# S5 products out of the state: four bands of 32 columns in two places of 96 records, read back on SyncE's queue

## The chip, the cores and the metric

The kernel runs on one core of a Trainium2 chip. The metric is the device time of one execution in microseconds, the median of several executions. The engines are named as in the profile: PE is TensorE (matmuls), DVE VectorE, ACT ScalarE, POOL GpSimd, SP SyncE (which here only issues DMAs).

## The reference

The network has two layers. A layer is a gated feed-forward part, a mixer, and a second gated feed-forward part, each on a normalised and modulated input, for 128 context tokens and 256 latent tokens (384 in all) of 1024 features. The change is in the mixer, whose input projection feeds three branches:

```
z = h @ w_in                                  # 512 + 512 + 512 columns
y_a = s5(z_a);  y_b = conv(z_b);  y_c = chunk_mlp(z_c)
gates = sigmoid(h @ w_gate + b_gate)          # 3 x 1024 columns
merged = g_a * (y_a @ w_br_a) + g_b * (y_b @ w_br_b) + g_c * (y_c @ w_br_c)
return merged @ w_out

def s5(z):                                    # 32 groups g of 16 channels, state of 64, both directions
    h[t] = abar_g * h[t-1] + bbar_g @ u[t]    # complex, forward; and the same backward
    y = sum over directions of Re(c_g @ h) + d * z
    y = gelu(y)
    return y * sigmoid(y @ w_glu)
```

All is float32. The three outputs are those of the context tokens, of the latent tokens, and the last S5 states of the context.

## The kernel before, in words

**Products.** Features lie on the partitions and the 384 tokens in the free dimension. A weight matrix is read in *units* of four k-tiles by 256 columns (128 x 1024 elements; those of w_br_c and w_br_b have two k-tiles, 128 x 512). A unit passes through four engines: SyncE loads it (`wr`, line 149), ScalarE rounds it to a short form (`wh`, L126), VectorE takes the rest (`wl` = `wr` - `wh`, L105), and TensorE makes three products for each k-tile and half of the columns (`mm3`, L198 to L200): `wh` by the high part of the input, `wh` by the low part, `wl` by the high part. There are three buffers each of `wr`, `wh` and `wl`, so the load of a unit may start when the `wl` three units earlier is made, and a `wh` when TensorE is done with the unit three before.

**Order in the mixer.** After w_in come the gate's third quarter and w_br_c by turns (two gate units, one of w_br_c, four times), then eight units of gate and so on. Beside this stream runs the rest of the mixer, written in `side()` as a plan with one step for each unit; its TensorE work goes into a queue `small` of *places*. After each `mm3` one place is taken from that queue and its matmuls stand there, between the large ones. TensorE's order is that in which the code is written. On the other engines, and in SyncE's queue of DMA issues, a scheduler at build time fixes the order. Each engine, and each queue, is then worked off strictly in that order.

**S5.** The 32 groups go in four quarters q of eight groups (GB = 8, GS = 4), and the 384 tokens as NCH = 48 chunks of TC = 8 tokens, so that a group's 16 channels times 8 tokens fill 128 partitions. For a quarter:

- `load_to(q)`: SyncE loads the rotation `m_rot`, the factors `m_rho` and two matrices `m_ms` (L1171).
- `to_state(q)`: the chunk's contribution to the state, `m_ms` by `U`, in two places (real and imaginary part), in four bands of 32 columns; ScalarE copies the result to `m_xs`.
- `rotate`, `scan`: VectorE turns the sequences (`m_t`), runs the recurrence as two scans over 400 elements, and turns back to `m_hh`.
- `load_from(q)`: SyncE loads `m_my` (two) and `m_mi` (L1254).
- `from_state(q)`: the output, `m_mi` by `U` and `m_my` by `m_hh`, summed in PSUM. ScalarE copies it out and writes it to `y_d` in DRAM; GpSimd reads it back as `m_yt`.
- `activate(t)`: adds d * z, applies gelu, and splits the result in `ah` and `al`, the input of the glu product.

The convolution's 31 taps for two halves (`cacc`, L123) are VectorE's filler between these.

Of the kernel before, what the change touches and what calls it, by code (L numbers as in the profile page):

```python
# [19 lines left out]
P = 128  # L20
# [36 lines left out]
def hybrid_step(ctx: ExitStack, tc: tile.TileContext, I, pos_r, pos_c, y_prompt, y_sample, new_state):  # L57
# [37 lines left out]
    def c2(shape, name):  # L95
        return sp.tile(shape, F32, tag="c2", name=name, bufs=7)
# [1021 lines left out]
    def mixer(l, ld, nxt):  # L1118
# [11 lines left out]


        zd = drm.tile([G, H, TC, NCH], F32, tag=f"z_d{l}", name="z_d")
        yd = drm.tile([NT, G * H], F32, tag=f"y_d{l}", name="y_d")
        ld.start()
        hs = ld.hs
        zp = m6([P, 4, NT], "zp")
# [43 lines left out]
        def to_state(q):  # L1180
            d = st5[q]
            gs = slice(q * GB, (q + 1) * GB)
            XS = c3([P, 2, GB, NE], "m_xs")
            d["xs"] = XS
            pool.memset(XS[:, :, :, 0:1], 0.0)
            act.activation(XS[:, :, :, EC], h0[:, :, gs], AF.Copy)

            def product(i, g, b):
                for r in range(0, P, 32):
                    pe.matmul(  # L1190
                        b[r : r + 32, g * NCH : (g + 1) * NCH],
                        d["ms"][g // GS][:, g % GS, i, r : r + 32],
                        U[:, q * GB + g, :],
                        start=True,
                        stop=True,
                        skip_group_check=True,
                    )

            def take(i, b):
                bv = b[:, : GB * NCH].rearrange("p (g c) -> p g c", c=NCH)  # L1200
                act.activation(XS[LO, i, :, 1:EC], bv[LO, :, :CC], AF.Copy)
                act.activation(XS[LO, i, :, EC + 1 :], bv[LO, :, CC:], AF.Copy)
                act.activation(XS[HI, i, :, 1:EC], bv[HI, :, CC - 1 :: -1], AF.Copy)
                act.activation(XS[HI, i, :, EC + 1 :], bv[HI, :, NCH - 1 : CC - 1 : -1], AF.Copy)

            for i in range(2):
                b = tb_bank()
                small.append([partial(product, i, g, b) for g in range(GB)] + [partial(take, i, b)])

        def rotate(q, part):  # L1210
            d = st5[q]
# [44 lines left out]
        def from_state(q):  # L1256
            d = st5[q]
            hh, mib = d["hh"], d["mi"]
            b = tb_bank()

            def product(g):
                for n in range(3):
                    for half in range(2):
                        i = 4 * half + g
                        u = U[:, q * GB + i, :] if n == 0 else hh[:, n - 1, i, :]
                        w = mib[:, i, :] if n == 0 else d["my"][i // GS][:, i % GS, n - 1, :]
                        pe.matmul(
                            b[64 * half : 64 * half + NCH, g * P : (g + 1) * P],
                            u,
                            w,  # L1270
                            start=(n == 0),
                            stop=(n == 2),
                            skip_group_check=True,
                        )

            def take():
                ysb = c2([P, TC, 4, H], "m_ysb")
                bv = b.rearrange("p (g i h) -> p i g h", g=4, h=H)
                yv = yd.rearrange("(c i) f -> c i f", i=TC)
                for half in range(2):  # L1280
                    r = slice(64 * half, 64 * half + NCH)
                    act.activation(ysb[r], bv[r], AF.Copy)
                    f0 = q * P + 64 * half
                    bq.dma_start(yv[:, :, f0 : f0 + 64], ysb[r].rearrange("c i g h -> c i (g h)"))
                d["yt"] = c2([P, 3, P], "m_yt")
                gq.dma_start(d["yt"], yd[:, q * P : (q + 1) * P].rearrange("(t p) f -> p t f", p=P))

            small.append([partial(product, g) for g in range(4)] + [take])

        def activate(t):  # L1290
            b = tb_bank()
            for n in range(3):
                transpose(b[:, n * P : (n + 1) * P], st5[t]["yt"][:, n, :], P)
            y2 = tmp("y2")
            ci = lambda v: v.rearrange("p (c i) -> p c i", i=TC)
            stt(ci(y2), zp[:, t].rearrange("p (j c) -> p c j", j=TC), pv[:, 48 + t : 49 + t], ci(b[:, :NT]))
            ga = tmp("ga")
            gelu_sig(ga, y2)
            yg = zp[:, t]
            mul(yg, y2, ga)  # L1300
            ygs[t] = yg
            hl = a_pair()
            split(yg, *hl)
            yas[t] = hl
# [183 lines left out]
        def side():  # L1488
            f = lambda fn, *a: (fn, a)
            tap = [f(conv_taps, j, min(j + 3, CONV_K)) for j in range(0, CONV_K, 3)]  # L1490
            plan = [
                [f(sg_weights)],
                [],
                [f(sg_bias)],
                [f(sg_u, 0), f(sg_u, 1)],
                [f(sg_gelu)],
                [f(to_state, 0), f(sg_norm)],
                [f(load_from, 0), f(rotate, 0, 0), f(rotate, 0, 1)],
                [f(load_to, 1), f(scan, 0, 0), f(sg_mix), f(sg_out)],
                [f(scan, 0, 1)],  # L1500
                [f(to_state, 1), tap[0]],
                [f(load_to, 2), f(rotate, 1, 0), f(rotate, 1, 1)],
                [f(from_state, 0), f(load_from, 1), f(scan, 1, 0)],
                [f(scan, 1, 1)],
                [f(to_state, 2), tap[1]],
                [f(load_to, 3), f(rotate, 2, 0), f(rotate, 2, 1)],
                [f(from_state, 1), f(load_from, 2), f(scan, 2, 0)],
                [f(scan, 2, 1)],
                [f(to_state, 3), tap[2]],
                [f(rotate, 3, 0), f(rotate, 3, 1)],  # L1510
                [f(from_state, 2), f(load_from, 3), f(scan, 3, 0)],
                [f(scan, 3, 1), f(activate, 0)],
                [tap[3]],
                [f(activate, 1)],
                [f(from_state, 3), tap[4]],
                [f(ctx_states), tap[5]],
                [f(activate, 2)],
                [tap[6]],
                [tap[7]],
                [f(activate, 3), tap[8]],  # L1520
                [tap[9]],
                [tap[10]],
                [f(conv_mean)],
                [f(conv_center)],
                [],
                [f(conv_var)],
                [],
                [f(conv_bcast)],
                [f(conv_scale)],
                [f(conv_out)],  # L1530
            ]
            for step in plan:
                for fn, a in step:
                    fn(*a)
                yield
# [312 lines left out]
```

## Time and profile before

| | |
|---|---|
| time before, median of 3 runs | 1773.07 us (1772.1 to 1774.9) |
| the profiled execution | 1772.74 us |
| its span in the trace | 1770.9 us |
| granted clock of TensorE, mean | 0.994 |
| TensorE busy | 98% |
| VectorE busy | 71% |
| ScalarE busy | 45% |
| GpSimd busy | 11% |

Busy shares are averages over the whole span; the mixer of the first layer lies around 350 to 570 us, that of the second 865 us later. In a timeline, a row is one instruction or a run of equal ones, with its start, its length, the engine, the line and what it makes from what; in brackets stands how long the engine sat idle before it and what released it. A letter q behind an engine's name (SPq) is its DMA issues. The matmuls of a place appear as two records each.

### The profile page before, as it was taken

How to read it: one execution, taken by the hardware profiler on the slowest of the kernel's cores; microseconds unless marked ns; L12 is line 12 of the kernel's file. 1: busy time of each engine (PE TensorE's matmuls, PEld its weight loads, DVE VectorE, ACT ScalarE, POOL GpSimd, SP SyncE). 2: the span in 40 equal slices, each digit the busy share in tenths (PEclk: the TensorE clock that was granted, in tenths of full speed). 3: DMA queues.
4: the chain of work that ended last, by engine and by line, in shares of the span. 5: the costliest groups of instructions: out<-in, count | busy, mean ns of one | idle time of the engine just before them, and what ended most of it. 6: DMA issues, size and time to landing. Idle time of an engine off the chain costs nothing.

```text
span 1770.9 us, 31161 instructions
## 1 busy us (share of the span) xinstructions
PE 1739.2 (98%) x12244; PEld 1660.3 (94%) x12244; DVE 1249.3 (71%) x2352; ACT 795.7 (45%) x1332; POOL 202.6 (11%) x400
## 2 busy tenths in 40 slices
PE   6999999999999999999999999999999999999997
PEld 4989989999999999999999999999999999999997
DVE  5495776888986986657787666677699688544445
ACT  3344333475355553233367333335744546323233
POOL 2012333410010000000001133222100000000000
PEclk9999999999999999999999999999999999999999
DMA  9679787676753567766745577757666443444342
GB/s 358 209 234 317 251 261 213 204 213 188 251 150 102 185 223 247 255 197 219 250 131 184 174 220 233 244 172 236 167 209 195 131 126 113 135 128 128 122 125 77
DMA packets 250298, 344.49 MB, mean 195 GB/s; under 512 B 22016, under 2 KB 216268, under 8 KB 250153
## 3 DMA queue, kind: packets, MB, share of 16 engines
q1 hardware_dynamic: 225048, 299.18, 53.1%
q0 software_dynamic: 17088, 39.51, 7.4%
q10 hardware_dynamic: 8016, 3.82, 0.8%
q8 instruction: 96, 1.57, 0.4%
q14 instruction: 50, 0.40, 0.1%
HBM read 309.75 MB, written 32.70 MB: 193 GB/s over the span
## 4 chain that ended last, share of the span: by engine, by line
PE 84%; DVE 10%; DMA 2%; ACT 2%; issue 1%; DVEq 0%; SPq 0%; ACTq 0%
PE mm L198 26%; PE mm L200 26%; PE mm L199 26%; PE ax L356 3%; DVE wl L105 2%; DVE cacc L123 2%; PE tb L138 1%; DVE m_t L105 1%; DMA wr<-in_w_in_dram 1%; DVE m_hh L105 1%; DMA wr<-in_w_gate_dram 1%; ACT wh L126 1%; PE tb L1042 0%; DMA modw<-in_w_mod_dram 0%; DVE acc L105 0%
## 5 line engine op out<-in xcount | busy, mean ns | idle before, releaser
L105 DVE TENSOR_TENSOR wl<-wr,wh 128x1024 fp32r<-128x1024 f32 (+2 forms) x389 | 457.0, 1175 | 335.7 <-ACT wh L126 333.9
L126 ACT ACTIVATE wh<-wr 128x1024 fp32r<-128x1024 f32 (+1 forms) x387 | 395.9, 1023 | 629.1 <-PE mm L199 444.6
L198 PE MATMUL mm<-hh,wh 128*128 128x384 f32 x1840 | 625.7, 340 | 5.0 <-ACT hh L639 5.0
L200 PE MATMUL mm<-hh,wl 128*128 128x384 f32 x1840 | 618.6, 336 | 5.7 <-DVE wl L105 5.5
L199 PE MATMUL mm<-hl,wh 128*128 128x384 f32 x1840 | 617.7, 336 | 0.2
L198 PEld LDWEIGHTS mm<-hh,wh 128*128 128x128 f32 x1840 | 347.2, 189 | 21.8 <-ACT wh L126 7.5
L200 PEld LDWEIGHTS mm<-hh,wl 128*128 128x128 f32 x1840 | 347.0, 189 | 8.3 <-DVE wl L105 8.2
L199 PEld LDWEIGHTS mm<-hl,wh 128*128 128x128 f32 x1840 | 347.2, 189 | 1.1 <-DVE hl L105 1.0
L198 PE MATMUL mm<-ah,wh 128*128 128x384 f32 x800 | 273.1, 341 | 0.0
L200 PE MATMUL mm<-ah,wl 128*128 128x384 f32 x800 | 270.1, 338 | 0.0
L199 PE MATMUL mm<-al,wh 128*128 128x384 f32 x800 | 269.4, 337 | 0.0
L198 PEld LDWEIGHTS mm<-ah,wh 128*128 128x128 f32 x800 | 150.3, 188 | 6.4 <-ACT wh L126 2.3
L199 PEld LDWEIGHTS mm<-al,wh 128*128 128x128 f32 x800 | 150.4, 188 | 0.6
L200 PEld LDWEIGHTS mm<-ah,wl 128*128 128x128 f32 x800 | 150.2, 188 | 0.0
L123 DVE SCALAR_TENSOR_TENSOR x<-mm,gt,x 128x128 f32<-128x128 f32 x224 | 83.3, 411 | 37.2 <-PE mm L200 37.1
L123 DVE SCALAR_TENSOR_TENSOR macc<-modw,silu_c,macc 128x1024 f32<-128x1024 f32 x56 | 70.0, 1279 | 21.4 <-DMA modw<-in_w_mod_dram 21.4
L198 PE MATMUL mm<-xh,wh 128*128 128x386 f32 x240 | 84.0, 350 | 0.0
L199 PE MATMUL mm<-xl,wh 128*128 128x386 f32 x240 | 81.4, 339 | 0.0
L200 PE MATMUL mm<-xh,wl 128*128 128x386 f32 x240 | 81.3, 339 | 0.0
L126 ACT ACTIVATE ah<-av 128x384 fp32r<-128x384 f32 x82 | 41.9, 517 | 82.3 <-DVE av L105 82.2
L123 DVE SCALAR_TENSOR_TENSOR cacc<-pad,pv,cacc 128x399 f32<-128x399 f32 x120 | 69.6, 627 | 0.0
L105 DVE TENSOR_TENSOR av<-mm,sg 128x384 f32<-128x384 f32 x76 | 42.1, 555 | 23.3 <-PE mm L200 23.0
(315 smaller groups left out, 1838.9 us busy)
## 6 DMA issues: line engine op xcount, KB each, us to landing
wr<-in_ffn_w_dram SPq DMA_DIRECT2D x256, 512.0 KB, 3.8
modw<-in_w_mod_dram SPq DMA_DIRECT2D x56, 768.0 KB, 5.7
modw<-in_w_mod_dram SPq DMA_DIRECT2D x56, 512.0 KB, 4.6
wr<-in_w_gate_dram SPq DMA_DIRECT2D x48, 512.0 KB, 3.6
wr<-in_w_in_dram SPq DMA_DIRECT2D x24, 512.0 KB, 4.6
my<-my POOLq DMA_DIRECT2D x16, 512.0 KB, 5.5
ms<-ms POOLq DMA_DIRECT2D x16, 512.0 KB, 5.5
m_ms<-ms SPq DMA_DIRECT2D x16, 512.0 KB, 7.0
```

Source lines behind the costliest of these rows:

```text
L105: (eng or dve).tensor_tensor(out, a, b, op=op)
L123: dve.scalar_tensor_tensor(out, a, s, b, op0=op0, op1=op1)
L126: act.activation(hi, full, AF.Copy)
L138: pe.transpose(out, in_, ident[:rows, :rows])
L198: pe.matmul(out, wh[:, k, cols], xh, start=first, stop=False)
L199: pe.matmul(out, wh[:, k, cols], xl, start=False, stop=False)
L200: pe.matmul(out, wl[:, k, cols], xh, start=False, stop=last)
L356: pe.matmul(b[32 * s : 32 * s + 32, :w], silu_c[:, k, :], raw[:, s * w : s * w + w], start=(k == 0), stop=(k == KD - 1), skip_group_check= ...
```

## The change

- `to_state`: both parts (real, imaginary) go into one place of the queue, 64 matmuls in a row.
- `from_state`: before, the stationary operand was `U` or `m_hh` (48 columns) and the moving one `m_mi` or `m_my` (128 columns), in one place of four steps. Now the stationary operand is a band of 32 columns of `m_mi` or `m_my` and the moving one `U` or `m_hh` (48 columns), in two places, four groups each. The result lies transposed to that of before.
- ScalarE copies one 128 x 384 block in place of two of 48 x 512, and writes `y_d` with one DMA in place of two.
- `load_y(q)`, new: `m_yt` is read with eight DMAs of 16 x 8 x 48 for each quarter, on SyncE's queue, in place of one DMA on GpSimd's. The plan has a step for it.
- `activate`: the three transposes are gone, since `m_yt` already lies with channels on the partitions; `y` is made from SBUF; the last multiply writes its result in token order.

```diff
-        yd = drm.tile([NT, G * H], F32, tag=f"y_d{l}", name="y_d")
+        yd = drm.tile([4, P, GB, NCH], F32, tag=f"y_d{l}", name="y_d")
...
+            place = []
             for i in range(2):
                 b = tb_bank()
-                small.append([partial(product, i, g, b) for g in range(GB)] + [partial(take, i, b)])
+                place += [partial(product, i, g, b) for g in range(GB)] + [partial(take, i, b)]
+            small.append(place)
...
                 for n in range(3):
-                    for half in range(2):
-                        i = 4 * half + g
-                        u = U[:, q * GB + i, :] if n == 0 else hh[:, n - 1, i, :]
-                        w = mib[:, i, :] if n == 0 else d["my"][i // GS][:, i % GS, n - 1, :]
+                    u = U[:, q * GB + g, :] if n == 0 else hh[:, n - 1, g, :]
+                    w = mib[:, g, :] if n == 0 else d["my"][g // GS][:, g % GS, n - 1, :]
+                    for r in range(0, P, 32):
                         pe.matmul(
-                            b[64 * half : 64 * half + NCH, g * P : (g + 1) * P],
+                            b[r : r + 32, g * NCH : (g + 1) * NCH],
+                            w[:, r : r + 32],
                             u,
-                            w,
...
-                ysb = c2([P, TC, 4, H], "m_ysb")
...
-                d["yt"] = c2([P, 3, P], "m_yt")
-                gq.dma_start(d["yt"], yd[:, q * P : (q + 1) * P].rearrange("(t p) f -> p t f", p=P))
-
-            small.append([partial(product, g) for g in range(4)] + [take])
+                ysb = c2([P, GB, NCH], "m_ysb")
+                act.activation(ysb, b[:, : GB * NCH].rearrange("p (g c) -> p g c", c=NCH), AF.Copy)
+                bq.dma_start(yd[q], ysb)
+
+            small.append([partial(product, g) for g in range(GS)])
+            small.append([partial(product, g) for g in range(GS, GB)] + [take])
+
+        def load_y(q):
+            d = st5[q]
+            d["yt"] = c2([P, TC, NCH], "m_yt")
+            for g in range(GB):
+                tq.dma_start(d["yt"][g * H : (g + 1) * H], yd[q, :, g, :].rearrange("(i h) c -> h i c", h=H))
...
-            for n in range(3):
-                transpose(b[:, n * P : (n + 1) * P], st5[t]["yt"][:, n, :], P)
             y2 = tmp("y2")
...
-            mul(yg, y2, ga)
+            mul(yg.rearrange("p (c i) -> p i c", i=TC), jc(y2), jc(ga))
...
-                [f(to_state, 2), tap[1]],
+                [f(to_state, 2), f(load_y, 0), tap[1]],
...
-                [f(to_state, 3), tap[2]],
+                [f(to_state, 3), f(load_y, 1), tap[2]],
...
-                [f(activate, 1)],
+                [f(load_y, 2), f(activate, 1)],
...
-                [f(activate, 2)],
+                [f(load_y, 3), f(activate, 2)],
```

SyncE's queue, before, in the first layer's mixer, from the load of c4 (the last unit of w_br_c in it) on; the two `m_ms` behind it are those of quarter 3, and the gate units that follow are g9 to g14:

```order
L149 DMA wr<-in_w_br_c_dram 128x2x256
L1171 DMA m_ms<-ms_128 128x1024 x2
L149 DMA wr<-in_w_gate_dram 128x4x256 x2
L1251 DMA m_my<-my_130 128x1024 x2
L1254 DMA m_mi<-mi_134 128x1024
L149 DMA wr<-in_w_gate_dram 128x4x256 x2
L1251 DMA m_my<-my_130 128x1024 x2
L149 DMA wr<-in_w_gate_dram 128x4x256 x2
L1254 DMA m_mi<-mi_134 128x1024
```

The same queue now, from the gate unit g9 on (g9, g10, g11 and g12 are its four loads):

```order
L149 DMA wr<-in_w_gate_dram 128x4x256
L1289 DMA m_yt<-y_d 16x8x48
L1165 DMA m_rot<-rot_136 128x800
L149 DMA wr<-in_w_gate_dram 128x4x256
L1167 DMA m_rho<-rhod_138 128x400
L1171 DMA m_ms<-ms_128 128x1024 x2
L1253 DMA m_my<-my_130 128x1024
L149 DMA wr<-in_w_gate_dram 128x4x256
L1253 DMA m_my<-my_130 128x1024
L149 DMA wr<-in_w_gate_dram 128x4x256
L1256 DMA m_mi<-mi_134 128x1024
```

The two `m_ms` of quarter 3 stood right behind c4 and now stand behind g10; the `m_mi` of quarter 2 stood behind g10 and now behind g12. Further on, from g13 to g16, the queue now reads:

```order
L149 DMA wr<-in_w_gate_dram 128x4x256
L1289 DMA m_yt<-y_d 16x8x48
L149 DMA wr<-in_w_gate_dram 128x4x256
L1289 DMA m_yt<-y_d 16x8x48 x4
L1253 DMA m_my<-my_130 128x1024
L149 DMA wr<-in_w_gate_dram 128x4x256
L1253 DMA m_my<-my_130 128x1024
L149 DMA wr<-in_w_gate_dram 128x4x256
L1256 DMA m_mi<-mi_134 128x1024
```

The `m_mi` of quarter 3, before behind g14, now stands behind g16, and reads of `m_yt` stand between the weight loads.

VectorE, before, from the `wl` of c3 (between the gate units g6 and g7) to that of g7, in the first layer; numbers in the names `m_t` tell buffers of a quarter apart:

```order
L105 TENSOR_TENSOR wl<-wr,wh 128x512
L123 SCALAR_TENSOR_TENSOR cacc<-pad,pv_311,cacc 128x399
L105 TENSOR_TENSOR m_t_5325<-m_rot,m_xs 128x400
L123 SCALAR_TENSOR_TENSOR cacc<-pad,pv_311,cacc 128x399 x2
L105 TENSOR_TENSOR m_t_5326<-m_rot,m_xs 128x400
L105 TENSOR_TENSOR m_t_5327<-m_rot,m_xs 128x400
L105 TENSOR_TENSOR m_t_5325<-m_t_5325,m_t_5326 128x400
L105 TENSOR_TENSOR m_t_5328<-m_rot,m_xs 128x400
L1233 SCALAR_TENSOR_TENSOR m_t_5326<-m_rho,m_t_5325 128x400
L105 TENSOR_TENSOR m_t_5327<-m_t_5327,m_t_5328 128x400
L105 TENSOR_TENSOR m_t_5325<-m_rot,m_t_5326 128x400
L105 TENSOR_TENSOR wl<-wr,wh 128x1024
```

The same stretch now, from the `wl` of g6 over those of c3 and g7 to that of g8 and what follows:

```order
L105 TENSOR_TENSOR wl<-wr,wh 128x1024
L105 TENSOR_TENSOR acc<-mm,gt 128x384
L105 TENSOR_TENSOR wl<-wr,wh 128x512
L105 TENSOR_TENSOR acc<-mm,gt 128x384
L123 SCALAR_TENSOR_TENSOR cacc<-pad,pv_311,cacc 128x399 x11
L105 TENSOR_TENSOR wl<-wr,wh 128x1024
L123 SCALAR_TENSOR_TENSOR cacc<-pad,pv_311,cacc 128x399 x6
L105 TENSOR_TENSOR wl<-wr,wh 128x1024
L123 SCALAR_TENSOR_TENSOR cacc<-pad,pv_311,cacc 128x399
L105 TENSOR_TENSOR acc<-mm,gt 128x384
L123 SCALAR_TENSOR_TENSOR cacc<-pad,pv_311,cacc 128x399 x2
L105 TENSOR_TENSOR m_t_5402<-m_rot,m_xs 128x400
```

The rotation and the first scan of quarter 2 (`m_t`) stood ahead of the `wl` of g7; now taps of the convolution stand there, and the rotation comes behind the `wl` of g8.

## Rows read from the trace of the kernel before

**Rows 1.** Windows: us, busy time (count) of PE, PEld, DVE, ACT, POOL, clock, DMA share, GB/s.

```profile
411.00:522.00 111.00, 108.34 (x1111) 102.87 (x1110) 110.36 (x208) 48.63 (x90) 8.86 (x16) 1.00 0.61 195
...
1276.00:1387.00 111.00, 107.98 (x1109) 102.52 (x1108) 110.34 (x208) 48.71 (x90) 3.96 (x8) 1.00 0.59 192
```

**Rows 2.** Timeline of PE: places, waits, and the first glu product.

```profile
462.44 0.89 PE L1190 MATMUL tb<-U,m_ms 128*32 128x48 f32 x64
...
470.86 0.45 PE L200 MATMUL mm<-hh,wl 128*128 128x384 f32 x1 [0.25 <-DVE wl L105]
...
488.60 0.45 PE L200 MATMUL mm<-hh,wl 128*128 128x384 f32 x1 [1.35 <-DVE wl L105]
...
493.14 0.43 PE L1267 MATMUL tb<-m_mi,U 128*48 128x128 f32 x4
...
531.27 0.65 PE L198 MATMUL mm<-ah,wh 128*128 128x384 f32 x1
```

**Rows 3.** Timeline of PE: three kinds of places and the matmuls around them.

```profile
403.53 0.34 PE L200 MATMUL mm<-hh,wl 128*128 128x384 f32 x1
...
403.79 0.89 PE L1190 MATMUL tb<-U,m_ms 128*32 128x48 f32 x64
...
404.89 0.33 PE L199 MATMUL mm<-hl,wh 128*128 128x384 f32 x1
...
432.44 0.43 PE L1267 MATMUL tb<-m_mi,U 128*48 128x128 f32 x4
...
435.47 0.33 PE L199 MATMUL mm<-hl,wh 128*128 128x384 f32 x1
...
477.76 0.49 PE L138 MATMUL tb<-ident,m_yt 128*128 128x128 f32 x3
...
478.26 0.34 PE L199 MATMUL mm<-hl,wh 128*128 128x384 f32 x1
```

**Rows 4.** Timeline of SyncE's queue.

```profile
449.72 0.88 SPq L1171 DMA_DIRECT2D m_ms<-ms  x2
...
462.34 0.38 SPq L1254 DMA_DIRECT2D m_mi<-mi  x1
...
480.40 0.45 SPq L1254 DMA_DIRECT2D m_mi<-mi  x1
```

**Rows 5.** Timeline of VectorE.

```profile
447.39 1.81 DVE L105 TENSOR_TENSOR wl<-wr,wh 128x1024 fp32r<-128x1024 f32 x2
...
453.19 0.98 DVE L1233 TENSOR_TENSOR_SCAN m_t<-m_rho,m_t 128x400 f32<-128x400 f32 x1
...
459.58 1.23 DVE L105 TENSOR_TENSOR wl<-wr,wh 128x1024 fp32r<-128x1024 f32 x1
...
463.35 1.25 DVE L105 TENSOR_TENSOR m_hh<-m_t,m_t 64x128 f32<-64x128 f32 x4
...
501.46 6.63 DVE L123 SCALAR_TENSOR_TENSOR cacc<-pad,pv,cacc 128x399 f32<-128x399 f32 x12
...
508.00 1.22 DVE L105 TENSOR_TENSOR wl<-wr,wh 128x1024 fp32r<-128x1024 f32 x1
...
511.31 0.90 DVE L123 SCALAR_TENSOR_TENSOR y<-zp,pv,tb 128x384 f32<-128x384 f32 x1
...
523.39 0.56 DVE L105 TENSOR_TENSOR al<-zp,ah 128x384 fp32r<-128x384 f32 x1 [0.59 <-ACT ah L126]
```

**Rows 6.** DMAs from issue to landing: first of the tile m_ms, then of m_mi.

```profile
DMA to landing us min/median/max: 4.7/7.0/8.6
...
DMA to landing us min/median/max: 5.6/7.0/8.3
```

**Rows 7.** Timeline of PE behind a long wait, and a window there.

```profile
43.28 0.69 PE L198 MATMUL mm<-hh,wh 128*128 128x384 f32 x1 [3.05 <-ACT hh L639]
...
49.31 0.48 PE L200 MATMUL mm<-hh,wl 128*128 128x384 f32 x1
...
43.00:46.00 3.00, 2.67 (x7) 2.27 (x8) 2.88 (x9) 1.90 (x5) 0.00 (x0) 0.50 1.02 386
```

More of the change, by code (lines that the diff above doesn't have):

```diff
@@ L1276, in take @@
             def take():
-                ysb = c2([P, TC, 4, H], "m_ysb")
[L1278 to L1284, printed above, removed]
-                d["yt"] = c2([P, 3, P], "m_yt")
-                gq.dma_start(d["yt"], yd[:, q * P : (q + 1) * P].rearrange("(t p) f -> p t f", p=P))
-            small.append([partial(product, g) for g in range(4)] + [take])
+                ysb = c2([P, GB, NCH], "m_ysb")
[8 more added lines that the diff above has]
+                tq.dma_start(d["yt"][g * H : (g + 1) * H], yd[q, :, g, :].rearrange("(i h) c -> h i c", h=H))
         def activate(t):
-            b = tb_bank()
-            for n in range(3):
-                transpose(b[:, n * P : (n + 1) * P], st5[t]["yt"][:, n, :], P)
             y2 = tmp("y2")
-            ci = lambda v: v.rearrange("p (c i) -> p c i", i=TC)
-            stt(ci(y2), zp[:, t].rearrange("p (j c) -> p c j", j=TC), pv[:, 48 + t : 49 + t], ci(b[:, :NT]))
+            stt(y2, zp[:, t], pv[:, 48 + t : 49 + t], st5[t]["yt"].rearrange("p i c -> p (i c)"))
             ga = tmp("ga")
```

## Prediction

> **What bounds the kernel now.** I read the windows first: over the middle of the mixer TensorE is busy 108.34 of 111 us in the first layer and 107.98 in the second, with VectorE busy 110.36 and 110.34 [rows 1]. The reader is to see two engines full at once: TensorE's own work is the time, and VectorE has nothing to spare in exactly the stretch that the change touches. Next the timeline of TensorE: it still stands 0.25 us ahead of the place of from_state(2) and 1.35 us later on, both times for `wl`, which VectorE makes [rows 2]. So a microsecond less on TensorE counts only where VectorE and the loads follow; and an order that makes VectorE or SyncE later can cost at once. The second layer repeats the first 864.97 us later, so I work out one mixer and double it. The profiled execution took 1772.74 us (span 1770.9 and 1.8 around it), 0.3 under the median; all sums start from 1772.7.
>
> **TensorE's own work.** A place of 64 records of to_state costs 403.79 to 404.89 less one usual spacing of 0.173: 0.93 us, and it begins 0.09 later than a matmul would [rows 3]. Two of them become one of 128: one start is saved, between 0 and 0.2 us; I take 0.2, since the start is seen in every place. from_state's 48 records cost 2.86 (432.44 to 435.47) [rows 3]. The new form, four bands of 32 columns with 48 moving ones, is to_state's form, which runs 64 records in 0.93: 96 records are 1.39, two places 2.79, plus one more start of 0.09. That is 2.88 for 2.86: nothing gained. Each activate loses three transposes, 0.33 us (477.76 to 478.26 less a spacing) [rows 3]. A quarter gives 0.53 us, a layer 2.1, both 4.2.
>
> The Trainium skill ("TensorE: Matmul & The Clock Gate", section "Wait — 56ns, not 53.3ns?") says that matmuls never start less than about 25 ns apart, however small. By that 96 records would be 2.4 us and a quarter 2.1 us dearer than now, some 17 us in all, as an estimate. The place of 64 records shows 14.5 ns a record, so here the measurement decides: the records of different bands run beside each other.
>
> **Work that is hidden.** The copy out of PSUM and the one write in place of two lie on ScalarE, which is not full (48.63 of 111 us [rows 1]). The eight reads of a quarter cost SyncE some 0.4 us each (an issue there takes 0.38 [rows 4]); they stand between weight loads that wait for VectorE anyway, until the order below. `y` reads 384 contiguous elements: I take 0.5 us in place of the 0.82 of now (0.90 at 511.31, [rows 5]), and the multiply into `zp` may pay that back; between them 0.3 gained and 0.35 lost, hidden, since the last `al` ends 8 us before the glu products (523.39 and 531.27 [rows 2, 5]). That margin is also what an 8 us delay of activate(3) alone would eat.
>
> **What is moved, and costs.** The orders shown with the change are the heart. SyncE is one queue: a load behind a weight load waits until that may start, and `wr` of a unit may start when VectorE has made `wl` three units earlier. I call the gate units g1 to g20 and the w_br_c units c1 to c4; each c stands behind every second g, so g10 waits for g8, g12 for g9 and g16 for g13. Before, both `m_ms` of quarter 3 are issued from 449.72, behind c4; now they stand behind g10 and m_rho. `m_mi` of quarter 2 goes from behind g10 (462.34) to behind g12, that of quarter 3 from behind g14 (480.40) to behind g16 [rows 4].
>
> So VectorE's new order sets them. From its rows a full `wl` costs 1.13 us (1.22 less the 0.09 by which durations overlap), a half one 0.59 (with a full one it makes the 1.81 at 447.39), a tap 0.545 (twelve from 501.46 to 508.00), a scan 0.90, a group of four m_hh 1.25, a 384-wide operation 0.47 and a 400-wide one 0.485 (an estimate by width) [rows 5]. `wl` of g6 starts near 447.0 (before 447.39: two acc go behind it, a tap goes ahead). Then 1.72 for it and c3, two acc 0.94, eleven taps 6.0: g7 at 455.7; 1.13 and six taps 3.27: g8 from 460.1 to 461.2. That is before's time (459.58 [rows 5]) almost exactly; but now the loads of `m_ms` stand behind it. Issues: g10 461.2, m_rho 461.6, m_ms 462.1 and 462.6.
>
> From 461.2 follow a tap, acc, two taps, five 400-wide operations, scan, two, scan, half `wl`, one, acc, m_hh, fin: 10.2 us, so `wl` of g9 runs 471.4 to 472.5, and g12 and m_mi(2) are issued at 472.6 and 473.0. To g13 follow twelve 400-wide operations 5.8, five taps 2.7, three m_hh 3.8, two scans 1.8, three `wl` 3.4, and acc, y, ga, zp, fin 3.2: 20.7 us. So g13 runs 493.2 to 494.4; g16 and m_mi(3) at 494.4 and 494.9.
>
> **The sum, for a layer.** (1) to_state(3): TensorE is there at 461.9 (462.44 [rows 2], less 0.4 by which `wl` of g6 comes sooner and 0.1 of places before). An m_ms lands 4.7 to 8.6 us after issue, median 7.0 [rows 6]; I take 6.5 for the second, since two loads go ahead of the pair: 469.1, with bounds 467.3 and 471.2. It is needed from the second half of the first 64 records on; 96 records remain, 1.4 us. TensorE leaves at 470.5, where before the same work was done at 464.3 (462.44 and two places): 6.2 late.
>
> (2) The clock. In the trace TensorE waited 3.05 us before 43.28, and the granted clock behind it is 0.50, which is 1.2 GHz; the 18 matmuls to 49.31 take 6.03 us where 18 spacings of 0.173 are 3.1: 2.9 lost [rows 7]. The wait of 1.35 us did no such thing: the granted clock of the whole stretch around it is 1.00 [rows 1, 2]. A wait of near 7 us is more than either, so I add 2.5 (0 to 2.9): 8.7. The wait of 0.25 goes [rows 2]: 8.45 late at from_state(2), which before starts at 471.2; so 479.7. m_mi lands 5.6 to 8.3 after issue [rows 6]; only one weight load stands just ahead of it, so I take 5.6: 478.6, in time. At the median of 7.0 it costs 0.4 more.
>
> (3) Between from_state(2) and from_state(3) two activates save 0.66 in transposes, and the 1.35 us wait goes, whose `wl` is early now: 6.4 late, from_state(3) at 499.6 (493.14 before [rows 2]). m_mi(3), again with one weight load ahead, lands at 500.5 (500.5 to 503.2): 0.9 of wait, 7.4 late. This load is a floor too: if less is lost before it, TensorE only waits longer for it.
>
> (4) Behind it two activates save 0.66: 6.7 late at the glu products. Behind them I know of no wait that could give it back. Twice 6.7 is 13.4: 1772.7 + 13.4 = **1786.1 us**.
>
> **Rivals.** *A. The loads stall TensorE (above), 1781 to 1793.* For it: the queue is in order, and VectorE has no gap in which it could reach g8 sooner. Chance 0.74.
>
> *B. The loads come in time, and VectorE's order alone paces.* If m_ms(3) landed by 462, from_state(2) would need m_hh of quarter 2, which the new order ends at 475.3 (2.8 us behind `wl` of g9): 4.1 late, less 1.35 and four times 0.33 behind it: 1.4 a layer, 1775.5; with the clock falling in that wait, 2.5 more a layer, 1780.5. Against it: issue to landing never went under 4.7 us [rows 6]. Chance 0.09.
>
> *C. Faster: the work saved on TensorE reaches the end.* One mechanism: VectorE runs the taps and `wl` ahead of g8 some 7 us faster than its rows give, and m_ms(3) is issued before 455.5, the point from which it decides. Then 2.1 a layer is gained, 1768.5, and with the two waits gone [rows 2] 1765.3. Against it: VectorE is busy 110.36 of 111 us [rows 1]. Chance 0.08.
>
> *D. The clock stays down.* If it fell at each of the three late loads (quarter 3 in, quarters 2 and 3 out), at 2.9 each, a layer costs 5 to 6 more: 1796 to 1798. The waits before the latter two are 0 and 0.9 in my sum, and 1.35 did nothing. Chance 0.06.
>
> *E. The bands don't run beside each other.* The row nearest is from_state's own: 2.86 us for 48 records with 128 moving columns, 60 ns each; 48 columns by that are 22 ns, a place 2.15, a quarter 1.4 dearer, 11 us over eight: 1797. Against it: the same form in to_state at 14.5 ns. Chance 0.03. (The skill's 25 ns above would be this case, and a little worse.)
>
> **Range and chances.** 1786.1 is A's value. About 0.2% (3.5 us) is what a measurement here can tell from no change. Downwards the floor of m_mi(3) holds it; there only VectorE's sum, which I give 2.5 us over the 47 of it, a layer, counts: 1781. Upwards m_mi(3) at 503.2 or m_ms(3) at 471.2 with the clock at 2.9 add 2.5 to 3.5 a layer: 1793. With half of B and little of D, 1777 to 1794 holds eight in ten. Faster by over 0.2%: C, 0.08. Within: part of B and the bottom of A, 0.06. Slower: 0.86.
>
> **What the profile after would show.** Right: TensorE idle 6 to 8 us ahead of to_state(3), near 462 and again 865 us later, released by the load of m_ms, with granted clock 0.50 behind it; m_ms(3) issued near 462 instead of 449.7; m_mi(2) near 473 and m_mi(3) near 495; a place of from_state of 1.4 us; the 1.35 us wait gone. Wrong if m_ms(3) is issued well before 460, if `wl` of g8 is reached at another time than 460, if a place takes 2 us, or if the stall at to_state(3) is there and is caught up before the glu products.

## The result, and the profile after

The changed kernel takes 1788.2 us (median of 4 runs, 1785.0 to 1793.7) against 1774.0 (1772.1 to 1775.1): a ratio of 1.009, 95% interval 1.0076 to 1.0104. It is slower, by 14 us; 1786.1 was forecast. The profiled execution, the fastest of the four, took 1785.0 us (span 1783.2), 12.2 more than that of before; what follows explains those 12.2.

First the waits of TensorE in the changed kernel (what it waited for: us in all, how many times, the longest). Before, it had none of these; it had 5.5 us of waits for `wl`, which are gone.

```profile
PE tb L1190 <- DMA m_ms<-ms: 11.7, 4, 7.1
PE tb L1268 <- issue: 5.3, 4, 2.0
...
PE tb L1268 <- DMA m_mi<-mi: 3.4, 3, 2.1
```

Next its timeline: to_state(3), the first product of c4, from_state(3) and the first glu product of the first layer, then to_state(3) and the first glu product of the second layer.

```profile
462.31 0.34 PE L200 MATMUL mm<-hh,wl 128*128 128x384 f32 x1
466.61 0.87 PE L1190 MATMUL tb<-U,m_ms 128*32 128x48 f32 x32 [3.96 <-DMA m_ms<-ms]
467.80 2.15 PE L1190 MATMUL tb<-U,m_ms 128*32 128x48 f32 x96 [0.33 <-DMA m_ms<-ms]
469.88 0.69 PE L198 MATMUL mm<-hh,wh 128*128 128x384 f32 x1
...
474.69 0.33 PE L198 MATMUL mm<-yc,wh 128*128 128x384 f32 x1
...
500.02 0.29 PE L1268 MATMUL tb<-U,m_mi 128*32 128x48 f32 x7 [2.14 <-DMA m_mi<-mi]
...
536.70 0.65 PE L198 MATMUL mm<-ah,wh 128*128 128x384 f32 x1
...
1340.66 0.87 PE L1190 MATMUL tb<-U,m_ms 128*32 128x48 f32 x32 [7.05 <-DMA m_ms<-ms]
...
1408.67 0.65 PE L198 MATMUL mm<-ah,wh 128*128 128x384 f32 x1
```

And before, the first product of c4 in the first layer and the first glu product of the second:

```profile
468.03 0.33 PE L198 MATMUL mm<-yc,wh 128*128 128x384 f32 x1
...
1396.24 0.65 PE L198 MATMUL mm<-ah,wh 128*128 128x384 f32 x1
```

The reader is to see: to_state(3), which ran at 462.44 without a wait before [rows 2], stands still for 3.96 and 0.33 us in the first layer and 7.05 and 0.33 in the second, each time for `m_ms`. The glu products start at 536.70 instead of 531.27 [rows 2]: 5.4 late, and 12.4 late in the second layer (1396.24 before), so 7.0 more there. The sum had 6.7 for each.

SyncE's queue in the changed kernel, first layer: `m_ms` of quarter 3, then `m_mi` of quarters 2 and 3.

```profile
460.93 0.86 SPq L1171 DMA_DIRECT2D m_ms<-ms  x2
...
471.69 0.43 SPq L1256 DMA_DIRECT2D m_mi<-mi  x1
...
493.77 1.39 SPq L1256 DMA_DIRECT2D m_mi<-mi  x1
```

They were issued at 449.72, 462.34 and 480.40 before [rows 4]. VectorE in the same kernel, the taps ahead of `wl` of g7, then that `wl` and that of g8:

```profile
448.25 6.08 DVE L123 SCALAR_TENSOR_TENSOR cacc<-pad,pv,cacc 128x399 f32<-128x399 f32 x11
454.24 1.22 DVE L105 TENSOR_TENSOR wl<-wr,wh 128x1024 fp32r<-128x1024 f32 x1
...
458.65 1.22 DVE L105 TENSOR_TENSOR wl<-wr,wh 128x1024 fp32r<-128x1024 f32 x1
```

`wl` of g8 was reached at 458.65 where 460.1 was worked out, with eleven taps and six more ahead of it. Last the windows (us, busy time and count of PE, PEld, DVE, ACT, POOL, then clock, DMA share, GB/s):

```profile
411.00:522.00 111.00, 100.75 (x1639) 96.10 (x1638) 106.66 (x202) 42.94 (x81) 5.85 (x12) 0.97 0.60 190
466.00:469.00 3.00, 2.06 (x92) 1.91 (x96) 3.00 (x7) 1.36 (x2) 0.00 (x0) 0.50 0.66 250
469.00:472.00 3.00, 3.00 (x55) 2.88 (x48) 2.97 (x7) 2.35 (x10) 0.00 (x0) 0.50 1.03 342
472.00:475.00 3.00, 3.00 (x18) 3.00 (x17) 2.96 (x9) 0.87 (x2) 0.00 (x0) 0.98 0.91 320
```

Behind the wait the granted clock is 0.50, that is 1.2 GHz. Over the whole stretch TensorE is busy 100.75 of 111 us, where it was 108.34 [rows 1], and VectorE is no longer full either.

### The profile page after: what moved, and what is told of

It is laid out like the page before. It is cut to its first block, busy times and chain, and to the rows that moved or that the text cites. A ratio compares the mean times of both kernels' runs of the same rounds, so it can differ in the third digit from the quotient of the medians.

```text
span 1783.2 us, 33437 instructions
## 1 busy us (share of the span) xinstructions
PE 1734.7 (97%) x13372; PEld 1657.1 (93%) x13372; DVE 1249.6 (70%) x2352; ACT 790.4 (44%) x1324; POOL 196.7 (11%) x392
## 4 chain that ended last, share of the span: by engine, by line
PE 90%; DVE 4%; DMA 2%; ACT 1%; issue 1%; SPq 0%; DVEq 0%; ACTq 0%
PE mm L198 28%; PE mm L199 27%; PE mm L200 27%; PE ax L356 3%; PE tb L138 1%; DMA m_mi<-mi 1%; DVE wl L105 1%; DVE cacc L123 1%; PE tb L1268 1%; DVE m_t L105 1%; PE tb L1190 1%; DMA wr<-in_w_in_dram 0%; PE tb L1042 0%; ACT wh L126 0%; DMA m_ms<-ms 0%
## 5 line engine op out<-in xcount | busy, mean ns | idle before, releaser
L356 PE MATMUL ax<-modw,silu_c 128*32 128x384 f32 (+2 forms) x704 | 58.6, 449 | 0.2 <-DMA modw<-in_w_mod_dram 0.2
```

The costliest lines, as they stand in the source:

```text
L356: pe.matmul(b[32 * s : 32 * s + 32, :w], silu_c[:, k, :], raw[:, s * w : s * w + w], start=(k == 0), stop=(k == KD - 1), skip_group_check= ...
```

## The experiments

Times are medians; each ratio is to the kernel before on the same chip. The first theory is that of the prediction: loads issued too late in SyncE's queue. Its rivals are VectorE's order by itself, and the short records, which bring a wait that I had not foreseen: 5.3 us "issue" inside places of from_state, where the profile names nothing that TensorE waits for.

**ly0_later.** One step of the plan altered, so that the reads of quarter 0 stand behind the loads of quarter 3.

```diff
-                [f(to_state, 2), f(load_y, 0), tap[1]],
-                [f(load_to, 3), f(rotate, 2, 0), f(rotate, 2, 1)],
+                [f(to_state, 2), tap[1]],
+                [f(load_to, 3), f(load_y, 0), f(rotate, 2, 0), f(rotate, 2, 1)],
```

> The changed kernel with one step of the plan altered: load_y(0) stands behind load_to(3) instead of ahead of it. By its order the two m_ms of quarter 3 are again issued behind c4, as before; m_mi of quarters 2 and 3 stay behind g12 and g16. Theory of late loads: the wait at to_state(3) (4.3 us in the first layer, 7.4 in the second) is gone; m_mi(2), issued near 469, lands near 475, 4 us after TensorE wants it, so that a wait of about 4 us turns up at from_state(2) and part of the loss stays: 1776 to 1784 us. If the first wait alone made the change slower: 1770 to 1775. If the short records and not the loads made it slower: as the changed kernel, 1785 to 1790.

1787.1 us, ratio 1.0087 (1.0070 to 1.0105); the profiled execution is the slowest of its four, 1790.9. Its waits, and its queue (`m_ms` of quarter 3, `m_mi` of quarter 2):

```profile
PE tb L1268 <- DMA m_mi<-mi: 10.1, 3, 6.0
PE tb L1268 <- issue: 6.4, 3, 2.7
```

```profile
450.70 0.89 SPq L1171 DMA_DIRECT2D m_ms<-ms  x2
...
473.64 0.43 SPq L1256 DMA_DIRECT2D m_mi<-mi  x1
```

`m_ms` is early again and its wait gone, and almost nothing is won: the wait now stands at from_state(2) for `m_mi`, 3.6 and 6.0 us long. The 1776 to 1784 expected was too low: the load was issued at 473.6 and not at 469, and the stalls without releaser grew to 6.4. The time alone would fit the third alternative, the short records; the waits do not, since 10.1 us of them are for a load.

**reads_pool.** The eight reads of a quarter on GpSimd's queue.

```diff
-                tq.dma_start(d["yt"][g * H : (g + 1) * H], yd[q, :, g, :].rearrange("(i h) c -> h i c", h=H))
+                gq.dma_start(d["yt"][g * H : (g + 1) * H], yd[q, :, g, :].rearrange("(i h) c -> h i c", h=H))
```

> The changed kernel with the eight reads of m_yt on GpSimd's queue, as the one read of before was. SyncE's queue then stands as before (m_ms(3) behind c4, m_mi(2) behind g10, m_mi(3) behind g14); the bands, the merged place and the missing transposes stay. Theory of late loads: all waits for m_ms and m_mi are gone, the clock stays at 1.00 in the mixer, and what is left is the gain of 4.2 us on TensorE and the stalls of 1 to 2 us inside from_state that the profile gives no releaser for (5.3 us in all): 1771 to 1776 us. Rival, the short records are what costs (stalls and more of them): 1780 or more.

1779.2 us, 1.0045 (1.0029 to 1.0060). Its waits:

```profile
PE tb L1268 <- issue: 8.4, 5, 2.6
```

No load stops TensorE any more, and VectorE's order is near that of before again. Of the 14 us some 9 are gone. What is left is above what I expected: the stalls have grown to 8.4 us.

**reads_pool_bands64.** The same, with half as many records.

```diff
-                    for r in range(0, P, 32):
+                    for r in range(0, P, 64):
...
-                            b[r : r + 32, g * NCH : (g + 1) * NCH],
-                            w[:, r : r + 32],
+                            b[r : r + 64, g * NCH : (g + 1) * NCH],
+                            w[:, r : r + 64],
```

> As reads_pool, and from_state in two bands of 64 columns instead of four of 32: 48 records a place instead of 96, half as many instructions. Theory that the stalls inside from_state come from how many instructions TensorE takes in a short time: they vanish (0 to 1 us left). A place costs 1.3 to 1.5 us if a 64-column record takes twice a 32-column one, 0.7 if it takes the same: 1766 to 1772. If the stalls come from a load or from another engine they stay near 5 us: 1771 to 1776.

1773.3 us, 1.0011 (1.0002 to 1.0021). Its waits:

```profile
PE tb L1268 <- DMA m_mi<-mi: 4.1, 2, 2.1
...
PE mm L200 <- DVE wl L105: 1.4, 2, 0.7
```

The stalls are gone altogether. The time lies in the second alternative all the same, above the expected 1766 to 1772, for two reasons: a new wait of 2 us a layer for `m_mi` of quarter 2, since the scheduler put that load behind g11, and dearer places. A place of 48 records of 64 columns takes 1.64 us (432.74 to 434.55 less a spacing of 0.173), where 96 records of 32 columns take 1.26 in the changed kernel and 1.3 to 1.5 was expected:

```profile
432.74 0.32 PE L1268 MATMUL tb<-U,m_mi 128*64 128x48 f32 x4
...
434.55 0.34 PE L199 MATMUL mm<-hl,wh 128*128 128x384 f32 x1
```

**to_state_alone.** The kernel before with the merged place of `to_state` alone.

> The kernel before with to_state's two places merged into one, nothing else. The start of a place is saved eight times, at most 0.2 us each: 1771.4 to 1773, the same within what can be told. If the merge itself reorders VectorE or the loads to a loss: 1776 or more.

1773.8 us, 1.0008 (0.9998 to 1.0017): the same. The merged place of 128 records, and the second matmul behind it:

```profile
402.97 1.57 PE L1190 MATMUL tb<-U,m_ms 128*32 128x48 f32 x128
...
404.74 0.33 PE L199 MATMUL mm<-hl,wh 128*128 128x384 f32 x1
```

1.60 us (1.77 less a spacing of 0.173) where two places took 1.86 and two late starts of 0.09 [rows 3]: 0.3 saved a quarter. In the profiled execution TensorE then waits 6.7 us for `wl` instead of 5.5 and gives about half of it back.

**changed_bands64.** The changed kernel, reads on SyncE's queue, with the two bands of 64 columns of above.

> The changed kernel, reads on SyncE's queue as there, with from_state in two bands of 64 columns. Its loads stand late as in the changed kernel (m_ms(3) behind g10, m_mi(2) behind g12, m_mi(3) near g16). If late loads and stalls inside from_state are two causes that add up: the stalls (5.3 us in the changed kernel's profile, about 6 with what the clock loses) go and the waits for m_ms and m_mi stay: 1779 to 1784 us, and no wait inside a place without a releaser. If the stalls were hidden behind the late loads: 1785 to 1790.

1785.6 us, 1.0079 (1.0061 to 1.0097). Its waits:

```profile
PE tb L1190 <- DMA m_ms<-ms: 12.6, 4, 6.4
...
PE tb L1268 <- DMA m_mi<-mi: 1.8, 2, 1.4
```

No stall without a releaser is left in from_state, and the kernel is only 2.6 us faster than the changed one, with the intervals overlapping. The time is that of the second alternative, but it doesn't show that the stalls were hidden. What lies ahead of to_state(3) is: in the first layer TensorE comes sooner and waits longer there (5.56 us against 3.96), and from_state(2) starts at 477.12 instead of 477.37. Over both layers, though, the waits for `m_ms` take back only 0.9 us (12.6 against 11.7), and those for `m_mi` fall. The larger part is the price of the new form: sixteen places at 1.64 us instead of 1.26 are 6.1 us, about what the stalls were. So this run doesn't tell whether the two causes add up.

Both of the next two start from reads_pool_bands64. **bands64_mi_first** loads `m_mi` ahead of `m_my`; **bands64_one_place** also puts the 96 records in one place (the last hunk).

```diff
             d["my"] = []
+            d["mi"] = c4([P, GB, P], "m_mi")
+            tq.dma_start(d["mi"], mi_d[l][:, q * GB : (q + 1) * GB])
             for s in range(2):
...
-            d["mi"] = c4([P, GB, P], "m_mi")
-            tq.dma_start(d["mi"], mi_d[l][:, q * GB : (q + 1) * GB])
...
-            small.append([partial(product, g) for g in range(GS)])
-            small.append([partial(product, g) for g in range(GS, GB)] + [take])
+            small.append([partial(product, g) for g in range(GB)] + [take])
```

> As reads_pool_bands64, with m_mi loaded ahead of the two m_my of a quarter. There TensorE waited 2.0 us for m_mi(2) in each layer and the clock took another 2 us. By its order m_mi(2) is now issued behind g9 and m_my behind g10 and g11, so the first place of from_state has its operands near 470. Theory of late loads: both waits go, 4 us a layer: 1764 to 1768 us, below the kernel before. If another wait takes their place (the second m_my, behind g11, lands near 472 for a place at 472): 1768 to 1773.

> As bands64_mi_first, with all 96 records of a quarter in one place of the queue instead of two of 48. One start of a place (0.1 to 0.2 us) is saved eight times, and the second m_my is wanted 1.9 us sooner. If that load has landed: 1763 to 1768 us; if not, a wait of 0.5 to 1 us a layer: 1766 to 1770.

1772.0 us, 0.9996 (0.9986 to 1.0005), and 1770.9 us, 0.9988 (0.9978 to 0.9997). In the first, only waits for `wl` are left in the mixer:

```profile
PE mm L200 <- DVE wl L105: 2.9, 6, 0.7
```

The wait for `m_mi` is gone; 1764 to 1768 was expected, and a gain of 4 us a layer did not come. The medians are 1.3 us apart, the profiled executions 3.4 (1772.35 and 1768.99, the latter the fastest of its ten); the waits for `wl` took back 1.5, and where the rest went stays open. Against the kernel before little can be left: its place of from_state took 2.86 us a quarter, two of 64-column records take 3.28, so of the 0.9 a quarter that the changed form saves on TensorE some 0.2 remain. In one place (the second kernel) the records take 3.04 in the trace. Its 1770.9 too is above what was expected.

**bands64_one_place_5**, the second kernel again in five rounds.

> bands64_one_place again, in five rounds, since its gain of 0.12% is near what a measurement can tell. If it is faster than the kernel before: 1768 to 1771 us with an interval below 1. If run to run spread made the gain: 1771 to 1774.

1772.2 us, 0.9995 (0.9986 to 1.0004). The gain is not confirmed: this version is as fast as the kernel before, not faster by what can be told.

**before_ms_late.** The kernel before with only the two `m_ms` of quarter 3 moved (`load_ms` is the loop over `m_ms` taken out of `load_to`, which calls it for the other quarters).

```diff
-                [f(scan, 2, 1)],
+                [f(load_ms, 3), f(scan, 2, 1)],
```

> The kernel before with one thing moved: the two loads of m_ms of quarter 3 are written two steps of the plan later, so that they stand behind g10 and m_mi(2) in SyncE's queue as they stand behind g10 in the changed kernel; bands, places, transposes and reads are those of before, and VectorE's order is nearly that of before. Theory of late loads: TensorE waits 5 to 7 us at to_state(3) in both layers, the granted clock falls to 0.50 behind it (2 to 3 us more), and the short waits for wl give back 1 to 1.6: 6 to 7 us a layer, 1782 to 1788 us. If a late m_ms alone is hidden or given back later: 1771 to 1775.

1785.6 us, 1.0069 (1.0054 to 1.0085). Its waits, and the window behind the first of them:

```profile
PE tb L1195 <- DMA m_ms<-ms: 14.0, 4, 7.1
```

```profile
472.00:476.00 4.00, 2.88 (x78) 2.13 (x71) 3.19 (x6) 1.08 (x4) 0.00 (x0) 0.50 0.64 197
```

This one move, with nothing else of the change, costs 12 us: 14.0 us of waits in the profile, and the clock at 0.50 behind them. (The profiled execution is the slowest of the four, 1789.7; it was already 3.7 us late at the first to_state of the mixer, 407.47 instead of 403.79.)

**bands64_loads_pool.** changed_bands64 with the loads of quarters 2 and 3 on GpSimd's queue, where no weight load stands ahead.

```diff
-                tq.dma_start(t, ms_d[l][:, q * GB + s * GS : q * GB + (s + 1) * GS])
+                (gq if q > 1 else tq).dma_start(t, ms_d[l][:, q * GB + s * GS : q * GB + (s + 1) * GS])
...
-                tq.dma_start(t, my_d[l][:, q * GB + s * GS : q * GB + (s + 1) * GS])
+                (gq if q > 1 else tq).dma_start(t, my_d[l][:, q * GB + s * GS : q * GB + (s + 1) * GS])
...
-            tq.dma_start(d["mi"], mi_d[l][:, q * GB : (q + 1) * GB])
+            (gq if q > 1 else tq).dma_start(d["mi"], mi_d[l][:, q * GB : (q + 1) * GB])
```

> As changed_bands64 (reads of m_yt on SyncE's queue), but m_ms, m_my and m_mi of quarters 2 and 3 are loaded on GpSimd's queue, where no weight load stands ahead of them. VectorE's order stays much as in the changed kernel: m_hh of quarter 2 ready near 475. If only the place of the loads in SyncE's queue made the changed kernel slow: 1769 to 1773 us. If VectorE's order alone paces once the loads come in time (the second rival of the prediction): a wait of 4 to 5 us at from_state(2), released by m_hh, 1775 to 1781. If neither: 1783 to 1787 as changed_bands64.

1783.9 us, 1.0063 (1.0050 to 1.0077). All loads are in time, and TensorE waits in the same place for another engine: 64 records of to_state(3) run at 462.59, the others from 469.10 on.

```profile
PE tb L1190 <- ACT m_ysb L1279: 11.3, 2, 5.7
```

```profile
462.59 0.89 PE L1190 MATMUL tb<-U,m_ms 128*32 128x48 f32 x64
...
469.10 1.51 PE L1190 MATMUL tb<-U,m_ms 128*32 128x48 f32 x64 [5.62 <-ACT m_ysb L1279]
```

```profile
467.54 0.98 DVE L1236 TENSOR_TENSOR_SCAN m_t<-m_rho,m_t 128x400 f32<-128x400 f32 x1
...
468.56 0.49 ACT L1279 ACTIVATE m_ysb<-tb 128x384 f32<-128x384 f32 x1 [2.63 <-DVE m_t L1236]
```

The last view has VectorE and ScalarE: ScalarE's copy `m_ysb` of quarter 1 frees the PSUM bank that to_state(3) needs for its second half, and that copy starts only when VectorE's second scan of quarter 2 (L1236) is done. (In the kernel `m_ysb` takes its buffer from the pool of seven in which `m_rho`, which the scan reads, and `m_t` lie; that it waits for such a buffer fits, and was not tried.) The copy waited for that scan before too, but the scan ran early:

```profile
456.18 0.98 DVE L1234 TENSOR_TENSOR_SCAN m_t<-m_rho,m_t 128x400 f32<-128x400 f32 x1
```

VectorE's new order puts that scan behind the `wl` of g8 and the taps ahead of it (ten and six in this run). So that order, with no load late, costs 11 us. Of the alternatives the time fits the last; the second had VectorE pacing by `m_hh` at from_state(2), which is not where the wait stands. In the changed kernel the same copy stands at nearly the time at which the last `m_ms` lands (467.80):

```profile
467.18 0.49 ACT L1279 ACTIVATE m_ysb<-tb 128x384 f32<-128x384 f32 x1 [8.74 <-DVE m_t L1236]
```

**reads_pool_spread** and **reads_pool_spread8**: from_state's places cut into four and into eight, to spread the 32-column records over more time.

```diff
-            small.append([partial(product, g) for g in range(GS)])
-            small.append([partial(product, g) for g in range(GS, GB)] + [take])
+            for g in range(0, GB - 2, 2):
+                small.append([partial(product, g), partial(product, g + 1)])
+            small.append([partial(product, GB - 2), partial(product, GB - 1), take])
```

> As reads_pool (four bands of 32 columns, 192 records a quarter), but in four places of 48 records with large matmuls between them, so that the same number of instructions is taken in 4.6 us instead of 2.9. If the stalls come from the rate at which TensorE takes instructions: the 8.4 us of stalls of reads_pool's profile fall to 0 to 4 us; two more starts a quarter cost 0.2 to 0.4 us, 2 to 3 us in all: 1773 to 1778 us. If the stalls belong to the form of the matmuls and not to the rate: still 7 to 9 us of stalls, 1780 to 1783.

> As reads_pool, but from_state in eight places of 24 records, one group each, so that a block of 256 instructions of TensorE takes about 4.4 us instead of 2.0 (reads_pool) or 3.0 (reads_pool_spread, whose stalls did not shrink). In the traces so far every stall stands at the same place in a block of 256, and the block's load lands 1.3 us before the stall ends, 2 to 5 us after TensorE began the block before. If TensorE only waits for the next block of instructions: stalls of 0 to 4 us in all against 8.4 and 10.0, and starts of places cost 0.1 to 0.2 us each (six more a quarter, 5 to 9 us in all): 1778 to 1786 us. If the stalls belong to the 32-column matmuls whatever their rate: 8 to 10 us of stalls, 1786 to 1792 us.

1784.8 us, 1.0064 (1.0049 to 1.0079), and 1784.0 us, 1.0060 (1.0043 to 1.0077). The stalls, of the one with four places and of the one with eight:

```profile
PE tb L1268 <- issue: 10.0, 6, 3.0
```

```profile
PE tb L1268 <- issue: 2.3, 2, 2.0
```

Four places did not shrink them (8.4 in reads_pool), against what I expected; eight did, though two stalls stay. That speaks for the rate and against the form of the records, but at a lower rate than I had taken. The total gains nothing by it, since `m_mi` is waited for again (2.8 and 3.5 us), and since a place costs more than I had taken. From one place of 24 records to the next in the kernel with eight:

```profile
434.20 0.29 PE L1268 MATMUL tb<-U,m_mi 128*32 128x48 f32 x8
...
435.31 0.29 PE L1268 MATMUL tb<-U,m_mi 128*32 128x48 f32 x8
```

That is 1.11 us, of which three large matmuls at 0.173 are 0.52: 0.59 for 24 records that take 0.255 inside a long place. A place costs 0.33 us beside its records, not 0.1 to 0.2, and six more a quarter are 2.0 us, 16 in all (an estimate from these rows).

## Why the prediction was right

*The late loads (1).* Right in mechanism and, over both layers, nearly in size. `m_ms` of quarter 3 was issued at 460.93 (462.1 worked out, since `wl` of g8 ran 1.5 us sooner than the sum had it) and ready at 467.80 (469.1). The prediction had named another time than 460 for that `wl` as a sign against it; the load was late all the same. The term was 6.2 us of delay and 2.5 for the clock, 8.7 a layer; between g8 and c4 TensorE fell back 6.6 us in the first layer (c4 starts at 474.69, before at 468.03; g8 0.1 late) and 9.5 in the second. The wait itself, forecast at 6 to 8 us in each layer, was 4.3 and 7.4. before_ms_late shows that this move alone makes the kernel 12 us slower.

*The clock (2).* Right: 0.50 from 466 to 472 in the changed kernel, and behind the waits of before_ms_late and ly0_later too. The size fits: from 466.61 to the start of the eighth large matmul behind the place, 472.23, pass 5.62 us, 0.33 of them a wait; a place of 1.60 and seven spacings of 0.173 would be 2.8, so 2.5 are lost. (The loss that it was taken from is 3.1 and not 2.9: 18 matmuls are 17 spacings apart.)

*m_mi as a floor (3).* Right in kind: waits of 2.14 us for quarter 3 in the first layer, 0.98 and 0.23 for quarters 2 and 3 in the second; from_state(3) starts at 500.02 where 500.5 was worked out. That less lost before such a load only makes the wait for it longer shows in ly0_later, there for `m_mi` of quarter 2.

*TensorE's own work.* The term was too small. A place of 96 records was taken at 1.39 us and takes 1.26, the merged place of to_state saves 0.3 instead of 0.2: 0.9 a quarter instead of 0.5, 3 us more over both layers. What made up for the error is the next point.

*What the sum did not have.* The changed kernel's places of from_state, the first of quarter 0 and, after two rows, the second:

```profile
431.17 0.29 PE L1268 MATMUL tb<-U,m_mi 128*32 128x48 f32 x8
...
432.60 0.33 PE L199 MATMUL mm<-hl,wh 128*128 128x384 f32 x1
...
433.83 0.27 PE L1268 MATMUL tb<-U,m_mi 128*32 128x48 f32 x8
436.11 0.38 PE L1268 MATMUL tb<-m_hh,m_my 128*32 128x48 f32 x16 [2.01 <-issue]
```

The second place stands 2.01 us in its midst. Four such stalls make 5.3 us, where the sum had none. Of these, 2.97 us (two stalls) lie ahead of to_state(3) in the first layer, where the wait hides them: without them the last `m_ms` is ready at 467.64 instead of 467.80 (changed_bands64). What the rest adds and what the sum missed of the gain on TensorE have opposite signs. That the forecast came within 2.1 us is therefore in part luck, as is that one layer was 1.3 under the 6.7 of the sum and the other 0.3 above.

*Rival B* was given 0.09 as "VectorE's order alone paces": its mechanism is there too, at another place and by another chain than I named, and bands64_loads_pool shows it worth 11 us by itself. The change is slower for two reasons, each enough for 11 to 12 us, that end at nearly the same moment (467.7 and 467.8 in the first layer, 1340.8 and 1341.9 in the second). So mending the loads alone gave nearly nothing (bands64_loads_pool against changed_bands64); mending VectorE's order alone in the changed kernel was not tried. Both come with the order in which the scheduler put VectorE's and SyncE's work once the reads stood on SyncE's queue. With the reads on GpSimd's queue both are gone. Why the scheduler chose that order was not looked into.

## What to carry to other kernels

Before a small DMA is put on a queue that also carries the loads of the critical path, read the order that results on every engine: here eight reads of 24 KB moved loads of 512 KB behind weight loads that wait for another engine, and one such move cost 12 us. Mend all chains that end at the same wait together; one by one they look worthless. When matmuls get so short that an engine takes hundreds of instructions in a few microseconds, count instructions too: half as many took away 6 us, though each place then took 1.64 us instead of 1.26.

## What the runs showed of the hardware

TensorE stalls for instructions. Counting its records (matmuls, weight loads and the few semaphore records between them) from the start of each trace, every stall without a releaser in from_state stands before a number that is 193 more than a multiple of 256 (6593, 7361, 8129, 19905, 20673 or 21441), in all five kernels with 32-column bands. In reads_pool one load of the instruction queue (q8; packets, MB, share) falls into the 2.5 us ahead of the first stall's end; it starts at 435.32 and takes 1.03:

```profile
q8 instruction: 1, 0.02, 2.6%
...
437.73 0.38 PE L1268 MATMUL tb<-m_hh,m_my 128*32 128x48 f32 x16 [2.57 <-issue]
```

Over the whole of a kernel this queue has about one packet for 256 records: 105 for 26,935 in reads_pool, 99 for 25,399 in reads_pool_bands64, 96 for 24,687 before.

Packet and stall belong together by number. 6593 is 25 times 256 and 193, and that stall ends behind the landing of the 25th packet; 21441 is 83 times 256 and 193, and that one ends behind the 83rd. So it is with all twenty stalls, each ending 1.26 to 1.58 us behind the landing.

The Trainium skill ("Runtime: NRT & Kernel Launch", section "Instruction fetch mechanics") says that instructions come in blocks of 256 by a DMA queue of the engine's own while the block before is worked off, and that the cost is mostly hidden. The block of 256 agrees with the stalls' places. "Mostly hidden" agrees by count, with five stalls for 105 blocks in reads_pool, but those five cost 8.4 us. From one such number to the next TensorE took, the stall included, 3.2 to 5.0 us at four of the five stalls of reads_pool and 9.6 at the fifth; in reads_pool_bands64 it took one block in 2.75 us without a stall. In the twenty cases the packet sets off 0.6 to 8.6 us after TensorE has passed the number 256 before. So the load's delay varies, and what decides it was not tried.

A record with four bands of 32 columns is cheaper by more than its width: 24 records take 0.255 us (431.45, 431.70 and 431.96 in the changed kernel), 10.6 ns each; with two bands of 64, twelve take 0.35 us (433.12 to 433.47 in reads_pool_bands64), 29 ns each:

```profile
433.12 0.29 PE L1268 MATMUL tb<-U,m_mi 128*64 128x48 f32 x4
...
433.47 0.29 PE L1268 MATMUL tb<-U,m_mi 128*64 128x48 f32 x4
```

Behind the stall of 2.57 us in reads_pool the granted clock fell (0.68 over the 3 us behind it); behind the one of 1.43 it stayed at 1.00, and behind that of 2.01 in the changed kernel too.
